# Turning q and k in the second layer by VectorE blocks and a scratch tile in DRAM in place of TensorE

## The chip, the cores and the metric

The kernel runs on one core of a Trainium2 chip. The metric is the device time of one execution in microseconds. Before: 2663.79 us, the median of three runs (2663.64 to 2665.55). Engines are named as in the profile: PE is TensorE's matmul, PEld its weight load, DVE VectorE, ACT ScalarE, POOL GpSimd, SP SyncE, which issues every DMA here.

## The reference, cut to what matters

An encoder trunk of two layers on 256 tokens of width 2048, in float32. In each layer:

```
h = rmsnorm(x) * (1 + sc_a) + sh_a                 # sc_a, sh_a: from c @ ada_w
qa, ka, va, qb, kb, vb, ga, gb = split(h @ w_in)   # qa 8 heads, ka/va 2, qb/kb/vb 8, of 128
qa, ka = rotary(rmsnorm(qa) * qn_a), rotary(rmsnorm(ka) * kn_a)
qb, kb = rmsnorm(qb) * qn_b, rmsnorm(kb) * kn_b
ya = window_attention(qa, ka, va, sink) @ w_proj_a
yb = neighbourhood_attention(qb, kb, vb, bias) @ w_proj_b
x = x + gt_a * ((sigmoid(ga) * ya + sigmoid(gb) * yb) @ w_out)
x = x + gt_m * ffn(x)                              # w_up, conv of width 3, silu gate, w_down
```

Scores are q k^T, so both q and k are wanted with the 128 entries of a head on the partitions and the tokens along the free dimension. The projection leaves them the other way, tokens on the partitions, because the norm of a head and the rotation run along the head's entries. Between the two lies a transposition ("turn") of each 128x128 block: 2 blocks of tokens for each head of q and k. That is what the change touches.

## The kernel before, in words

**Weights.** All weights of a layer stand in DRAM in the order of their use, in units of 16 blocks of 128x128 (1 MB). `unit_steps` (L280) loads a unit (L286) into one of four buffers "raw", and splits it, in two halves of 8 blocks, into a high and a low part: ACT casts (L297), DVE subtracts (L298). The halves are called hl and have four buffers, so two units can lie split ahead. Every product is three matmuls: high by high, high by low, low by high. Loads of ada_w (aw, L225, also 1 MB and also in "raw") stand between those of the units; DVE reduces each against c (L226).

**Order of the work.** `Stream.next_block` (L338) hands out blocks; at the end of each unit `tick` (L331) runs `bg.tick` (L258): first what was deferred at the tick before, then background jobs, each at a rate of steps per tick. The attention of a layer is such a job (L842): one step moves each live head on by one stage and takes in the next head, at 0.4 steps per tick in the second layer (`ATT`, L81). Heads 0 to 7 are those of mixer A, and may start when `ready` (L851) says that the groups they need are turned; the heads of mixer B follow. The program so written is then laid out by a scheduler, engine by engine: each engine has one list that it works off in order, and waits on semaphores for the others. SP's list holds all the DMAs. A DMA holds one of eight semaphores until it has landed.

**The stage of the change.** In the second layer, units 8 to 43 are nine groups of 512 columns of `w_in`, four units each (`Stream.tokens`, L367): group 0 holds k of mixer A (2 heads) and v, 1 and 2 q of mixer A, 3 and 6 k and 5 and 8 q of mixer B with four heads each, 4 and 7 v of mixer B. Units 0 to 7 before and 44 to 51 after them are the gate of mixer A, then comes its projection.

For each group of q or k, `qk_rows` (L539) runs in deferred steps:

- ACT squares each head's rows and sums them (L547), DVE and POOL make the reciprocal roots (L440, L441);
- three ticks later `norm` (L553) scales into the tile qn, 128 tokens x 2 x 4 heads x 128 (L556), and rotates q and k of mixer A (L571 to L573). qn has one buffer;
- one tick later `turn` (L576): for each of two blocks of tokens TensorE transposes each head (L580) into a PSUM tile qtp, and ACT copies that, scaled by the gain, into `dst` (L581), a part of packA or packB. Then `ready` is raised.

**Attention**, `attend` (L602), in stages of one step: q and k are split into high and low (`in_halves`, L588: ACT L389, DVE L390); six matmuls make the scores sc (L607), DVE adds mask or bias and takes the row maxima (L610) and negates them (nm, L615), ACT takes exponentials (L618, with es for the sink, L621), DVE adds and inverts (den L622, ri L624), ACT scales (L626). One step later four transpositions on TensorE (tp, L631), a split of the turned p into pT (L389, L390; one buffer), and one step later six matmuls with v (po, L639) and a split of o (L641, L642). tp, sc, po and qtp share three PSUM buffers "ax". This path of p is as before in both kernels.

Of the kernel before, what the change touches and what calls it, by code (L numbers as in the profile page):

```python
# [15 lines left out]
P = 128  # L16
L = 2
D = 2048
S = 256
# [8 lines left out]
NEG = -1e30  # L28
SCALE = HEAD ** -0.5
GRID_W, NA_KH, NA_KW = 64, 8, 16  # L30


QKV_GROUPS = [1024, 0, 512, 2560, 3584, 1536, 3072, 4096, 2048]
# [48 lines left out]
ATT_B = [0.21, 0.21]  # L82

SCORES_3 = (1,)

ADA_ORDER = [[p * KC + k for k in range(KC) for p in ps] for ps in ((0, 1), (2,), (3, 4), (5,))]
ADA_ORDER = [i for part in ADA_ORDER for i in part]
# [47 lines left out]
def encoder(ctx: ExitStack, tc: tile.TileContext, a: dict, out: bass.AP):  # L135
# [16 lines left out]
    sm = pool("sm", 3)  # L152
    mm = pool("mm", 4, space=bass.MemoryType.PSUM)
    ax = pool("ax", 3, space=bass.MemoryType.PSUM)

    ident = const.tile([P, P], F32, name="ident")
    make_identity(nc, ident[:])
# [228 lines left out]
    def split(dst, src, scale=None):  # L386

        if scale is None:
            nc.scalar.copy(dst[:, 0], src)  # L389
            nc.vector.tensor_tensor(out=dst[:, 1], in0=src, in1=dst[:, 0].bitcast(F32), op=ALU.subtract)  # L390
            return
        nc.scalar.activation(out=dst[:, 0], in_=src, func=AF.Copy, scale=scale)
        nc.vector.scalar_tensor_tensor(
            out=dst[:, 1], in0=src, scalar=scale, in1=dst[:, 0].bitcast(F32), op0=ALU.mult, op1=ALU.subtract
        )
# [140 lines left out]
            nc.vector.tensor_tensor(out=z[:], in0=ps[:, :S], in1=self.rbs[:], op=ALU.mult)  # L536
            return z, sh

    def qk_rows(pss, heads, rot, gain, dst, then):  # L539

        cols = 0
        n = heads * HEAD
        ss = sm.tile([P, 8], F32, name="qss", tag="qss")
        for t, ps in enumerate(pss):
            for i in range(heads):
                sq = at.tile([P, HEAD], F32, name="qsq", tag="qsq", bufs=1)
                nc.scalar.activation(  # L547
                    out=sq[:], in_=ps[:, cols + i * HEAD : cols + (i + 1) * HEAD], func=AF.Square,
                    accum_out=ss[:, t * heads + i : t * heads + i + 1],
                )  # L550
        rs = sm.tile([P, 8], F32, name="qrs", tag="qrs")
        rsqrt(rs[:, : 2 * heads], ss[:, : 2 * heads], HEAD, 2 * heads)
        def norm():  # L553
            qn = at.tile([P, 2, 4, HEAD], F32, name="qn", tag="qn", bufs=1)
            for t, ps in enumerate(pss):
                nc.vector.tensor_tensor(  # L556
                    out=qn[:, t, :heads],
                    in0=ps[:, cols : cols + n].rearrange("p (h d) -> p h d", d=HEAD),
                    in1=rs[:, t * heads : (t + 1) * heads].unsqueeze(2).broadcast_to([P, heads, HEAD]),
                    op=ALU.mult,  # L560
                )
            if rot is not None:
                x1, x2 = qn[:, :, :heads, :HALF], qn[:, :, :heads, HALF:ROT]
                tab = [rot[:, i].unsqueeze(2).broadcast_to([P, 2, heads, HALF]) for i in range(4)]
                tm = []
                for i in range(2):
                    z = ev.tile([P, S], F32, name=f"rt{i}", tag="z")
                    z = z[:].rearrange("p (i t h d) -> p i t h d", i=2, t=2, h=4)
                    tm += [z[:, 0, :, :heads], z[:, 1, :, :heads]]
                for i, src in enumerate((x1, x2, x2, x1)):  # L570
                    nc.vector.tensor_tensor(out=tm[i], in0=src, in1=tab[i], op=ALU.mult)  # L571
                nc.vector.tensor_tensor(out=x1, in0=tm[0], in1=tm[1], op=ALU.subtract)
                nc.vector.tensor_tensor(out=x2, in0=tm[2], in1=tm[3], op=ALU.add)  # L573
            bg.defer(lambda: turn(qn))

        def turn(qn):  # L576
            for t in range(2):
                ps = ax.tile([P, 4, P], F32, name="qtp", tag="ax")
                for h in range(heads):
                    nc.tensor.transpose(ps[:, h], qn[:, t, h], ident[:])  # L580
                nc.scalar.activation(  # L581
                    out=dst[:, :, t * P : (t + 1) * P], in_=ps[:, :heads], func=AF.Identity, scale=gain
                )
            then()

        bg.defer(lambda: bg.defer(lambda: bg.defer(norm)))
# [12 lines left out]

        return ((0, 0), (0, 1), (1, 0))[: 2 * len(x) - 1]  # L600

    def attend(q, k, v, p, mask, scale, sink, o):  # L602

        sc = ax.tile([P, 2, S], F32, name="sc", tag="ax")
        for t in range(2):
            for i, j in by(q):
                nc.tensor.matmul(sc[:, t], q[i][:, t * P : (t + 1) * P], k[j], start=i + j == 0, stop=(i, j) == by(q)[-1])  # L607
        m = sm.tile([P, 2], F32, name="m", tag="m")
        for t in range(2):
            nc.vector.tensor_tensor_reduce(  # L610
                out=p[:, t], in0=sc[:, t], in1=mask[:, t], scale=scale, scalar=-3.0e38 if sink is None else sink,
                op0=ALU.add, op1=ALU.max, accum_out=m[:, t : t + 1],
            )
        nm = sm.tile([P, 2], F32, name="nm", tag="nm")
        nc.vector.tensor_scalar(out=nm[:], in0=m[:], scalar1=-1.0, scalar2=None, op0=ALU.mult)  # L615
        den = sm.tile([P, 2], F32, name="den", tag="den")
        for t in range(2):
            nc.scalar.activation(out=p[:, t], in_=p[:, t], func=AF.Exp, bias=nm[:, t : t + 1], accum_out=den[:, t : t + 1])  # L618
        if sink is not None:
            es = sm.tile([P, 2], F32, name="es", tag="es")  # L620
            nc.scalar.activation(out=es[:], in_=nm[:], func=AF.Exp, bias=sink)  # L621
            nc.vector.tensor_tensor(out=den[:], in0=den[:], in1=es[:], op=ALU.add)  # L622
        ri = sm.tile([P, 2], F32, name="ri", tag="ri")
        nc.vector.reciprocal(out=ri[:], in_=den[:])  # L624
        for t in range(2):
            nc.scalar.activation(out=p[:, t], in_=p[:, t], func=AF.Copy, scale=ri[:, t : t + 1])  # L626
        yield
        tp = ax.tile([P, 2, S], F32, name="tp", tag="ax")
        for k in range(2):
            for t in range(2):  # L630
                nc.tensor.transpose(tp[:, k, t * P : (t + 1) * P], p[:, t, k * P : (k + 1) * P], ident[:])  # L631
        pT = at.tile([P, 2, 2, S], F32R, name="pT", tag="pT", bufs=1)
        split(pT, tp[:])
        v = v()
        yield
        po = ax.tile([P, 512], F32, name="po", tag="ax")
# [121 lines left out]
    for l in range(L):  # L758
# [112 lines left out]
        for pi, (groups, gates) in enumerate(parts):  # L871
            last = pi == len(parts) - 1
            for g, part in enumerate(groups):
                have_h(part)
                pss = st.tokens(h, part)
                if pi == max(0, len(parts) - 2) and g == 0:
                    gains, sink, cw, rots = small(l)
                dst = packs[g // 3][:, 4 * (g % 3) : 4 * (g % 3) + 4]
                rows = dst.rearrange("p (t a) s -> p t (a s)", t=2)
                if not last or pi > 0:  # L880
                    for t, ps in enumerate(pss):
                        if pi == 0:
                            nc.scalar.copy(rows[:, t], ps[:])
                        else:
                            nc.vector.tensor_tensor(out=rows[:, t], in0=ps[:], in1=rows[:, t], op=ALU.add)
                    pss = [rows[:, t] for t in range(2)]
                if not last:
                    continue

                def turned(g=g):  # L890
                    ready[0] = g + 1

                vcol = {0: GA * HEAD, 4: 0, 7: 0}.get(g)
                if vcol is not None and pi == 0:
                    for t in range(2):
                        nc.scalar.copy(rows[:, t, vcol:], pss[t][:, vcol:])
                if g == 0:
                    qk_rows(pss, GA, rots[1], gains[:, 1:2], kTa, turned)
                elif g < 3:
                    qk_rows(pss, 4, rots[0], gains[:, 0:1], dst, turned)  # L900
                elif vcol is None:
                    qk_rows(pss, 4, None, gains[:, 3:4] if g in (3, 6) else gains[:, 2:3], dst, turned)
                else:
                    turned()
                if g == 2:
                    bg.add(job, ATT[l])
# [242 lines left out]
```

## Time and profile before

| | |
|---|---|
| median of 3 runs | 2663.79 us |
| the profiled execution | its page gives a span of 2663.2 us and no time beside it |
| granted TensorE clock | full throughout (9 in all 40 slices) |
| DMA | 700.41 MB in 102,039 packets, mean 263 GB/s |
| packets under 512 B | 12,721 |
| written to DRAM | 2.10 MB, the output |
| chain that ended last | PE 89%, DVE 6%, ACT 1%, DMA 1%, issue 1% |

The profile is of one execution. Times of an instruction are its start from the start of the span and its duration. A busy TensorE is not a TensorE at its peak: matmuls overlap, and the distance from one start to the next tells the rate. "Idle before" in square brackets is time in which that engine had nothing to do, and the arrow names what ended it. The view of the chain of waits follows, from the last instruction back, what each one waited for.

### The profile page before, as it was taken

What the parts mean: (1) busy time and instruction counts of PE and PEld (TensorE: products, weight loads), DVE (VectorE), ACT (ScalarE), POOL (GpSimd) and SP (SyncE); (2) the same over time, 40 slices, a digit from 0 to 9 for tenths busy, and PEclk for the clock granted to TensorE, in tenths of its full rate; (3) what the DMA queues carried; (4) which work ended last, traced back from release to release, by engine and by line L of the source; (5) the groups of instructions that cost most, each with busy time, mean ns of one, the idle gap of its engine ahead of it and who ended that gap; (6) DMA issues with size and microseconds to landing.
All of it is one profiled execution on the core that took longest, in us unless ns stands there. A gap on an engine that the chain in (4) does not pass through costs nothing.

```text
span 2663.2 us, 50845 instructions
## 1 busy us (share of the span) xinstructions
PE 2650.9 (100%) x21256; PEld 2565.7 (96%) x21256; DVE 2102.2 (79%) x2959; ACT 1412.8 (53%) x2284; POOL 36.2 (1%) x25
## 2 busy tenths in 40 slices
PE   9999999999999999999999999999999999999999
PEld 7888899999999999999998889999999999999999
DVE  8898998997987888788976667768888866655664
ACT  5445865456644555355555566554565445544553
POOL 0001100000000000000000000000000000000000
PEclk9999999999999999999999999999999999999999
DMA  9987789885787878788766666666747765555554
GB/s 372 351 327 292 262 300 352 317 320 199 291 294 287 302 288 295 289 294 289 290 217 254 228 229 231 245 252 253 285 173 288 297 256 190 190 194 194 197 191 143
DMA packets 102039, 700.41 MB, mean 263 GB/s; under 512 B 12721, under 2 KB 15025, under 8 KB 17969
## 3 DMA queue, kind: packets, MB, share of 16 engines
q1 hardware_dynamic: 101810, 697.17, 71.4%
q8 instruction: 166, 2.72, 0.4%
q14 instruction: 63, 0.52, 0.1%
HBM read 695.03 MB, written 2.10 MB: 262 GB/s over the span
## 4 chain that ended last, share of the span: by engine, by line
PE 89%; DVE 6%; ACT 1%; issue 1%; DMA 1%; POOL 0%; SPq 0%; DVEq 0%; ACTq 0%
PE ps L314 25%; PE ps L316 25%; PE ps L315 25%; PE ps_t L377 4%; PE ps_t L379 4%; PE ps_t L378 4%; DVE hl L298 2%; DVE aw L226 2%; DMA aw<-in_aw 1%; PE sc L607 1%; PE po L639 1%; ACT hl L297 1%; PE tp L631 1%; POOL qrs L441 0%; PE qtp L580 0%
## 5 line engine op out<-in xcount | busy, mean ns | idle before, releaser
L298 DVE TENSOR_TENSOR hl<-w,hl 128x1024 fp32r<-128x1024 f32 x928 | 1128.3, 1222 | 360.0 <-ACT hl L297 357.6
L297 ACT CAST hl<-w 128x1024 fp32r<-128x1024 f32 x928 | 970.7, 1049 | 748.5 <-PE ps L316 518.1
L314 PE MATMUL ps<-h,hl 128*128 128x256 f32 x3328 | 922.8, 277 | 1.3 <-DVE ya L915 0.6
L315 PE MATMUL ps<-h,hl 128*128 128x256 f32 x3328 | 919.8, 276 | 0.0
L316 PE MATMUL ps<-h,hl 128*128 128x256 f32 x3328 | 919.8, 277 | 0.0
L314 PEld LDWEIGHTS ps<-h,hl 128*128 128x128 f32 x3328 | 624.8, 188 | 2.4 <-DVE ya L915 0.8
L315 PEld LDWEIGHTS ps<-h,hl 128*128 128x128 f32 x3328 | 625.3, 188 | 0.4 <-DVE h L470 0.2
L316 PEld LDWEIGHTS ps<-h,hl 128*128 128x128 f32 x3328 | 624.4, 188 | 0.0
L226 DVE CUSTOM_DVE_ANT_0 aw<-aw,cact,ab 128x2048 f32<-128x2048 f32 x189 | 443.5, 2347 | 48.8 <-DMA aw<-in_aw 47.8
L377 PE MATMUL ps_t<-hl,h 128*128 128x512 f32 x576 | 223.1, 392 | 2.6 <-ACT h L469 2.1
L378 PE MATMUL ps_t<-hl,h 128*128 128x512 f32 x576 | 224.9, 391 | 0.3
L379 PE MATMUL ps_t<-hl,h 128*128 128x512 f32 x576 | 224.3, 390 | 0.0
L994 DVE SCALAR_TENSOR_TENSOR u<-ps,cw,u 128x255 f32<-128x255 f32 x304 | 146.1, 481 | 66.5 <-ACT u L992 62.2
L992 ACT ACTIVATE u<-ps,cw 128x256 f32<-128x256 f32 x152 | 85.9, 565 | 187.9 <-PE ps L316 187.5
L316 PE MATMUL ps<-merged,hl 128*128 128x256 f32 x512 | 141.8, 277 | 0.4 <-DVE hl L298 0.4
L315 PE MATMUL ps<-merged,hl 128*128 128x256 f32 x512 | 141.6, 277 | 0.0
L314 PE MATMUL ps<-merged,hl 128*128 128x256 f32 x512 | 141.6, 277 | 0.0
L315 PE MATMUL ps<-act_o,hl 128*128 128x256 f32 x512 | 141.4, 276 | 0.0
L316 PE MATMUL ps<-act_o,hl 128*128 128x256 f32 x512 | 141.3, 276 | 0.0
L314 PE MATMUL ps<-act_o,hl 128*128 128x256 f32 x512 | 141.2, 276 | 0.0
L377 PEld LDWEIGHTS ps_t<-hl,h 128*128 128x128 f32 x576 | 107.9, 188 | 26.1 <-ACT h L469 3.1
L378 PEld LDWEIGHTS ps_t<-hl,h 128*128 128x128 f32 x576 | 108.1, 188 | 23.7 <-DVE hl L298 1.9
(231 smaller groups left out, 4612.5 us busy)
## 6 DMA issues: line engine op xcount, KB each, us to landing
w<-in_ws SPq DMA_DIRECT2D x463, 1024.0 KB, 4.9
aw<-in_aw SPq DMA_DIRECT2D x189, 1024.0 KB, 6.1
p<-in_bias SPq DMA_DIRECT2D x16, 256.0 KB, 4.2
x<-in_xT SPq DMA_DIRECT2D x4, 512.0 KB, 5.3
aw_o<-in_aw SPq DMA_DIRECT2D x2, 1024.0 KB, 12.3
out<-x SPq DMA_DIRECT2D x16, 128.0 KB, 2.1
w<-in_ws SPq DMA_DIRECT2D x2, 512.0 KB, 11.7
aw_b<-in_aw SPq DMA_DIRECT2D x1, 1024.0 KB, 18.1
```

Of the source, the lines that this page charges most:

```text
L226: nc.vector.tensor_tensor_reduce(out=raw[:], in0=raw[:], in1=cact[:], scale=1.0, scalar=ab[:, i : i + 1], op0=ALU.mult, op1=ALU.add, accum ...
L297: nc.scalar.copy(hl[:, 0], r)
L298: nc.vector.tensor_tensor(out=hl[:, 1], in0=r, in1=hl[:, 0].bitcast(F32), op=ALU.subtract)
L314: nc.tensor.matmul(out, hi, act[0], start=first, stop=False)
L315: nc.tensor.matmul(ps[:, :S], hi, act[1], start=False, stop=False)
L316: nc.tensor.matmul(out, lo, act[0], start=False, stop=last)
L377: nc.tensor.matmul(ps[:], xh, hi, start=kc == kcs[0], stop=False)
L378: nc.tensor.matmul(ps[:], xh, lo, start=False, stop=False)
L379: nc.tensor.matmul(ps[:], xl, hi, start=False, stop=kc == kcs[-1])
L607: nc.tensor.matmul(sc[:, t], q[i][:, t * P : (t + 1) * P], k[j], start=i + j == 0, stop=(i, j) == by(q)[-1])
L992: nc.scalar.activation(out=u, in_=ps, func=AF.Identity, scale=w[:, 1:2], bias=w[:, 3:4])
L994: nc.vector.scalar_tensor_tensor(out=u[:, to], in0=ps[:, of], scalar=w[:, j : j + 1], in1=u[:, to], op0=ALU.mult, op1=ALU.add)
```

## The change

A list `MOVED = (1,)` names the layers of the change, so the first layer stays as it is. In the second layer `turn` no longer uses TensorE and PSUM. For each of the two blocks of tokens VectorE transposes qn in place, which it does in blocks of 32x32, each block for itself. To bring the blocks to their places, eight DMAs per group (two blocks of tokens by four groups of 32 partitions) store qn into a scratch tile qY in DRAM, 128 x heads x 256, in runs of 32 elements (128 B). One tick later one DMA loads qY into `dst`, and one tick after that ACT scales `dst` in place by the gain, and `ready` is raised. The DRAM tile has two buffers. The code for p in `attend` has the same path as an option, which no caller takes. `once` serves that option alone.

```
+BLOCK = 32
+MOVED = (1,)
...
+    dram = pool("dram", 2, space=bass.MemoryType.DRAM)
...
+    def scatter(y, src, t, a):
+
+        rows = y[:].rearrange("(b i) n (t a j) -> t a i n b j", i=BLOCK, t=2, a=P // BLOCK)
+        nc.sync.dma_start(rows[t, a], src[a * BLOCK : (a + 1) * BLOCK])
+
-    def qk_rows(pss, heads, rot, gain, dst, then):
+    def qk_rows(pss, heads, rot, gain, dst, then, moved=False):
...
         def turn(qn):
+            if moved:
+                flat = qn[:, :, :heads].rearrange("p t h d -> p t (h d)")
+                for t in range(2):
+                    nc.vector.transpose(out=flat[:, t], in_=flat[:, t])
+                y = dram.tile([P, heads, S], F32, name="qY", tag="qY")
+                for t in range(2):
+                    for a in range(4):
+                        scatter(y, qn[:, t, :heads].rearrange("p h (b j) -> p h b j", j=BLOCK), t, a)
+
+                def back():
+                    nc.sync.dma_start(dst, y[:])
+
+                    def scaled():
+                        nc.scalar.activation(out=dst, in_=dst, func=AF.Identity, scale=gain)
+                        then()
+
+                    bg.defer(scaled)
+
+                bg.defer(back)
+                return
             for t in range(2):
                 ps = ax.tile([P, 4, P], F32, name="qtp", tag="ax")
...
-                    qk_rows(pss, GA, rots[1], gains[:, 1:2], kTa, turned)
+                    qk_rows(pss, GA, rots[1], gains[:, 1:2], kTa, turned, l in MOVED)
...
-                    qk_rows(pss, 4, rots[0], gains[:, 0:1], dst, turned)
+                    qk_rows(pss, 4, rots[0], gains[:, 0:1], dst, turned, l in MOVED)
```

The two groups of mixer B's q and k are called with `l in MOVED` likewise.

More of the change, by code (lines that the diff above doesn't have):

```diff
@@ L600, in by, with once, run, attend @@
         return ((0, 0), (0, 1), (1, 0))[: 2 * len(x) - 1]
-    def attend(q, k, v, p, mask, scale, sink, o):
+    def once(fn):
+        due = [fn]
+        def run():
+            if due:
+                due.pop()()
+        return run
+    def attend(q, k, v, p, mask, scale, sink, o, moved=False):
         sc = ax.tile([P, 2, S], F32, name="sc", tag="ax")
@@ L627, in attend @@
         yield
-        tp = ax.tile([P, 2, S], F32, name="tp", tag="ax")
-        for k in range(2):
+        if moved:
+            flat = p[:].rearrange("p t k -> p (t k)")
+            nc.vector.transpose(out=flat, in_=flat)
+            y = dram.tile([P, 2, S], F32, name="pY", tag="pY")
             for t in range(2):
-                nc.tensor.transpose(tp[:, k, t * P : (t + 1) * P], p[:, t, k * P : (k + 1) * P], ident[:])
-        pT = at.tile([P, 2, 2, S], F32R, name="pT", tag="pT", bufs=1)
-        split(pT, tp[:])
+                for a in range(4):
+                    scatter(y, p[:, t].rearrange("p (k b j) -> p k b j", k=2, j=BLOCK), t, a)
+            yield
+            pT = at.tile([P, 2, 2, S], F32R, name="pT", tag="pT", bufs=1)
+            whole = pT[:, 1].bitcast(F32)
+            nc.sync.dma_start(whole, y[:])
+            halve = once(lambda: split(pT, whole))
+            bg.defer(halve)
+        else:
+            tp = ax.tile([P, 2, S], F32, name="tp", tag="ax")
+            for k in range(2):
+                for t in range(2):
+                    nc.tensor.transpose(tp[:, k, t * P : (t + 1) * P], p[:, t, k * P : (k + 1) * P], ident[:])
+            pT = at.tile([P, 2, 2, S], F32R, name="pT", tag="pT", bufs=1)
+            split(pT, tp[:])
         v = v()
         yield
+        if moved:
+            halve()
         po = ax.tile([P, 512], F32, name="po", tag="ax")
@@ L897, in encoder @@
                 if g == 0:
-                    qk_rows(pss, GA, rots[1], gains[:, 1:2], kTa, turned)
+                    qk_rows(pss, GA, rots[1], gains[:, 1:2], kTa, turned, l in MOVED)
                 elif g < 3:
-                    qk_rows(pss, 4, rots[0], gains[:, 0:1], dst, turned)
+                    qk_rows(pss, 4, rots[0], gains[:, 0:1], dst, turned, l in MOVED)
                 elif vcol is None:
-                    qk_rows(pss, 4, None, gains[:, 3:4] if g in (3, 6) else gains[:, 2:3], dst, turned)
+                    qk_rows(pss, 4, None, gains[:, 3:4] if g in (3, 6) else gains[:, 2:3], dst, turned, l in MOVED)
                 else:
```

## The prediction

> **What bounds the kernel now.** I read the page first (which engine is full), then the view of busy time by stretches for the second layer's q/k/v stage, then that stage's timeline. In the page's line the columns are busy time, share and instructions; in the stretch view they are the stretch, its length, busy time and count for PE, weight load, DVE, ACT and POOL, granted clock, DMA share and GB/s.
>
> ```profile
> PE 2650.9 (100%) x21256; PEld 2565.7 (96%) x21256; DVE 2102.2 (79%) x2959; ACT 1412.8 (53%) x2284; POOL 36.2 (1%) x25
> 1394.00:1640.00 246.00, 245.94 (x1295) 211.02 (x1294) 165.29 (x251) 144.09 (x308) 10.91 (x7) 1.00 0.65 241
> ```
>
> TensorE is never without work in this stage (245.94 of 246.00 us, clock 1.00), DVE is at 67%, ACT at 59%, the DMA engines at 65%. So whatever leaves TensorE is gained, and whatever makes TensorE wait is lost in full: nothing later has slack to give it back.
>
> ```profile
> 1483.00 0.39 PE L378 MATMUL ps_t<-hl,h 128*128 128x512 f32 x1
> 1483.23 0.39 PE L379 MATMUL ps_t<-hl,h 128*128 128x512 f32 x1
> 1483.46 1.03 PE L580 MATMUL qtp<-ident,qn 128*128 128x128 f32 x8
> 1484.25 0.48 PE L377 MATMUL ps_t<-hl,h 128*128 128x512 f32 x1
> 1484.56 0.39 PE L378 MATMUL ps_t<-hl,h 128*128 128x512 f32 x1
> L580 PE MATMUL qtp<-ident,qn x52: 270/272/273, 1438.5 to 1631.8; 128*128 128x128 f32 x52
> ```
>
> The timeline's first column is the start. Durations overlap; the pitch counts: 0.23 us from one 512-column matmul to the next, so a unit (24 of them in this stage) takes 5.44 us and a group of four units 21.8 us.
>
> **What is removed.** From 1483.46 to 1484.56 there are eight turns and one matmul: 1.10 - 0.23 = 0.87 us for eight, 0.109 each. The last row (instructions of tile qtp in this stage) counts 52. Gain on TensorE: 52 x 0.109 = **5.7 us**, all on the path. [...]
>
> **Durations for what follows**, from the timeline of head 0 of mixer A and its neighbours (start, duration, engine, line):
>
> ```profile
> 1491.86 1.29 DVE L556 TENSOR_TENSOR qn<-ps_t,qrs 128x512 f32<-128x512 f32 x2 [1.81 <-POOL qrs L441]
> 1506.36 0.59 ACT L896 COPY packB<-ps_t 128x512 f32<-128x512 f32 x1
> 1506.95 0.95 PE L607 MATMUL sc<-kA,qA 128*128 128x256 f32 x6
> 1507.94 0.48 DVE L610 CUSTOM_DVE_ANT_0 p<-sc,maskA,sink 128x256 f32<-128x256 f32 x1 [2.00 <-PE sc L607]
> 1508.35 0.48 DVE L610 CUSTOM_DVE_ANT_0 p<-sc,maskA,sink 128x256 f32<-128x256 f32 x1
> 1508.75 2.35 DVE L226 CUSTOM_DVE_ANT_0 aw<-aw,cact,ab 128x2048 f32<-128x2048 f32 x1
> 1511.03 0.17 DVE L615 TENSOR_SCALAR nm<-m 128x2 f32<-128x2 f32 x1
> 1511.10 0.42 DVE L390 TENSOR_TENSOR qA<-packA,qA 128x256 fp32r<-128x256 f32 x1
> 1513.08 0.51 ACT L618 ACTIVATE p<-p,nm 128x256 f32<-128x256 f32 x1
> 1514.08 0.28 ACT L621 ACTIVATE es<-nm,sink 128x2 f32<-128x2 f32 x1
> 1514.39 0.16 DVE L622 TENSOR_TENSOR den<-den,es 128x2 f32<-128x2 f32 x1 [0.60 <-ACT es L621]
> 1514.59 0.17 DVE L624 RECIPROCAL ri<-den 128x2 f32<-128x2 f32 x1
> 1515.21 0.90 ACT L626 ACTIVATE p<-p,ri 128x256 f32<-128x256 f32 x2
> 1516.16 1.05 ACT L297 CAST hl<-w 128x1024 fp32r<-128x1024 f32 x1
> 1517.24 1.23 DVE L298 TENSOR_TENSOR hl<-w,hl 128x1024 fp32r<-128x1024 f32 x1 [0.68 <-ACT hl L297]
> 1518.68 0.60 PE L631 MATMUL tp<-ident,p 128*128 128x128 f32 x4
> 1519.04 0.96 PE L607 MATMUL sc<-kA,qA 128*128 128x256 f32 x6
> 1519.84 0.58 ACT L389 CAST pT<-tp 128x512 fp32r<-128x512 f32 x1
> 1521.11 0.69 DVE L390 TENSOR_TENSOR pT<-tp,pT 128x512 fp32r<-128x512 f32 x1
> ```
>
> The 14 evictions of qtp on ACT go too, and seven scalings in place come (128x1024 each, as the cast at 1516.16: 1.05 us, 7.4 us if nothing covered them). ACT's idle 41% covers them, and I cost them at nothing outside the chains that follow.
>
> **What is added on the queues.** Per group of four heads: two DVE turns of 128x512, which no row shows; below by nothing, above by two of the 2.35 us of a 128x2048 operation, and I take the 128x512 row at 1521.11 (0.69 us), so 1.4 us. Then eight stores of 512 pieces of 128 B, and one load back of 512 rows of 1 KB. In all 6.5 such groups: 26,624 pieces. The nearest row for a store to DRAM is the end of the run, where two stores of 128 rows of 1 KB are alone (the last 8.2 us; 288 packets with their 32 semaphore writes):
>
> ```profile
> q1 hardware_dynamic: 288, 0.26, 9.1%
> out<-x SPq DMA_DIRECT2D x2, 128.0 KB, 1.8
> w<-in_ws SPq DMA_DIRECT2D x463, 1024.0 KB, 4.9
> 1471.37 0.33 SPq L225 DMA_DIRECT2D aw<-in_aw  x1
> 1475.11 5.94 SPq L286 DMA_DIRECT2D w<-in_ws  x3
> ```
>
> So 0.091 x 16 x 8.2 / 288 = 41 ns a packet. A piece of 128 B lies between an eighth of that (5 ns, if bytes count) and 41 ns (if packets count); I take 41, the row of a store. A group's stores are then 4096 x 41 / 16 = 10.5 us of all engines, the load back 1.3 us; over the stage 77 us, against 35% of 246 = 86 us that are free. It fits, closely. SP issues a DMA in 0.33 us, so eight are 2.6 us, beside the transfer.
>
> Where the stores stand on SP matters: in the built program they come before loads that today go ahead of them, and the load back waits until all eight have landed, with the next loads behind it. The loads of units 26 to 28 are issued here from 1475.11 on; in the changed program that of unit 28 stands behind the stores of group 3, whose data exist only after that group's norm (1491.86 above). But unit 28 is due only around 1505 (1484.25 - 0.87 + 21.8), the load lands in 4.9 us, and the joint below makes TensorE later still. Walked through with 10.5 us per group, only unit 23 comes late by itself. Its load stands behind group 1's stores:
>
> ```profile
> 1446.37 1.29 DVE L556 TENSOR_TENSOR qn<-ps_t,qrs 128x512 f32<-128x512 f32 x2 [1.53 <-POOL qrs L441]
> 1448.70 0.89 DVE L571 TENSOR_TENSOR rt<-qn,rot 128x128 f32<-128x128 f32 x4
> ```
>
> In the new DVE list, from 1446.37 on: norm 1.3, rotation 1.4, one reduction of aw 2.35, four subtractions 4.9 and two turns 1.4, together 11.3: the second turn ends at 1457.7. Stores begin after the first turn, near 1456, and have landed near 1468.5 (10.5 and 1.8). The load back and unit 23's load leave then and land near 1475; cast and subtraction (1.05 + 1.23) make 1477.3, and the unit is due at 1476.7 (1483.46 - 5.44 - 1.3 for the turns gone): late by about **1 us**. The other loads are late by less than the waits that come next, and hide behind them.
>
> **What is moved: the attention steps.** This is the large term. The engines run their lists in order, and the lists of the changed kernel are another mix. TensorE's, with the number of matmuls:
>
> ```
> before: units 24-27, turns x8, sc0 x6, 28, 29, tp0 x4, sc1 x6, 30, 31, 32,
>         po0 x6, tp1 x4, sc2 x6, 33, 34, po1, tp2, sc3, 35 ...
> after:  unit 23 with sc0 x5 inside, 24, sc0 x1, tp0 x1, sc1 x3, 25 (sc1 x1 inside), tp0 x3, sc1 x2,
>         26 (po0 x2 inside), 27, po0 x4, tp1 x4, sc2 x6, po1 x6, tp2 x1, sc3 x3, tp2 x3, sc3 x3, 28, po2, 29-37,
>         tp3, sc4, po3, 38, 39, tp4, sc5, po4, tp5, sc6, po5 x2, 40 (po5 x4 inside), tp6, sc7,
>         41 (po6 x2 inside) ...
> ```
>
> Before, two or three units (11 to 16 us) lie between the scores of a head (sc), its turn (tp) and its product (po). After, whole heads stand back to back at the joints 24/25, 27/28, 37/38 and 39/40, and the DVE and ACT lists hold the split of the next unit's weights (hl) *behind* the softmax of the last head. What one head takes is in the rows of head 0 above. On TensorE tp takes 0.36 us (1518.68 to 1519.04), and sc and po, six matmuls each, about 0.8. Each joint's wait is the chain to the next unit's first hl, less TensorE's own work in it:
>
> - 24/25. Unit 24's end frees sc0's last matmul; then second reduction 0.48, qA and nm 0.5, group 3's norm 1.29 and its two DVE turns 1.4 (they stand ahead in DVE's list; ACT's exponentials run beside them), den and ri 0.37, scaling 0.45, cast 1.05, subtraction 1.23: 6.8, less 0.6 of tp and sc: **6.2 us**.
> - 25/26. A reduction 0.48 and the subtraction 1.23 behind it: 1.7; inside unit 26 po0 waits for pT behind a second subtraction, 1.23 + 0.69 - 0.45: 1.5. **3.2 us**.
> - 27/28. Two evictions 1.2 (L896), one o copy 0.4 (as qA's), pT 0.58 + 0.69, two reductions 0.9, qA and nm 0.5, exponentials with es 1.28 (1513.08 to 1514.36), den and ri 0.37, scaling 0.90, cast 1.05, subtraction 1.23: 9.1 plus about 0.5 for the hand-overs, less 3.6 of TensorE's work: **6.0 us**.
> - 28/29. pT, aw's 2.35, three small ones and the split in DVE's list against 5.44 + 0.8 of TensorE: **1.6 us**.
> - 37/38. pT 1.3, two reductions 0.9, subtraction 1.23, behind tp: 4.0 less 1.7: **2.3 us**.
> - 39/40. As 27/28, with a second pT (0.69) ahead of the split: 10.4 less 3.4: **7.0 us**.
> - 40/41. aw's reduction stands ahead of den: scaling, split and po6's pT come **3.3 us** late.
>
> Sum 29.6, with unit 23's 1 us 30.6, less 5.7 gained: **+24.9 us** on the profiled execution's span of 2663.2 us, so 2688.1. The median of the runs shown, 2663.79, is 0.6 above that span; added, **2689 us**. These are chains put together from one execution; each may be off by a third, and the loads could arrive during the joints later than walked.
>
> **The rivals.**
>
> *Pieces dearer than any row* (the queue becomes the bound). At 82 ns, twice the dearer end, the stores and loads back are 136 + 9 = 145 us beside 160 us (0.65 x 246) of the present traffic: the stage would need 305 us, 59 more, and the joints' waits disappear in that: 2663.8 + 59, some 2723 us. For it: SP sends one queue in order, and 128 B is far below every load's row. Against: nothing in the trace shows a small store costing more than a large one. [...]
>
> *The turns leave and nothing waits* (the other side). The place is TensorE's list, the price -5.7 us: 2658.1. It decides once the joints' waits stay below 0.4 us in all, which needs softmax, turn and product of a head to follow within the 3.6 us of matmuls at 27/28. Head 0's rows speak against it: from 1513.08 to 1516.11 alone are exponentials and scaling.
>
> *Half the joints.* If the waits of the two joints without a full softmax (25/26, 37/38) and half of the others don't appear, 12 us stay: 2663.8 + 12 + 1 - 5.7 = 2671.
>
> **How the numbers follow.** Forecast (2689, with its waits uncertain by a third: 2679 to 2699) 0.60; dearer pieces 0.17; half the joints 0.15; nothing waits 0.03; in between, waits and gain about equal, 0.05. A measurement of this kernel can tell about 0.2%, 5.3 us, from no change. The range goes from 2671 (the half case in) to 2724 (the dear case in). Faster 0.03, same 0.05, slower 0.92.
>
> **What would show it.** Right: in the profile after, TensorE falls below 100% in the stage only at the joints named, with idle time ended by DVE's hl and ACT's pT; no qtp row; the stage's DMA share near 0.9. The pieces' price shows in the queue's packets and its share. Wrong: idle TensorE ended by loads (w) spread over the stage means the dearer pieces; a TensorE without gaps means that the joints' chains run beside more than I saw. A stretch longer outside 1394 to 1700 would be a cause that I missed altogether.

## The result, and the profile after

The changed kernel takes 2687.07 us (median of 4, 2685.47 to 2688.46), the kernel before, beside it on the same chip, 2663.93 us: 23.1 us more, ratio 1.0084 (95% interval 1.007 to 1.0097). The forecast was 2689. It hits the time and the places. Two of its large terms are wrong, though, and that they cancel is luck; the section after the experiments takes them one by one.

The page of the changed kernel (span 2686.4 us of an execution of 2688.46), and the view by stretches for the stage of the change, with the columns of before:

```profile
PE 2660.2 (99%) x21204; PEld 2568.8 (96%) x21204; DVE 2108.7 (78%) x2973; ACT 1411.1 (53%) x2277; POOL 37.6 (1%) x25
```

```profile
1394.00:1640.00 246.00, 231.15 (x1052) 190.53 (x1051) 155.77 (x239) 132.02 (x279) 12.08 (x7) 0.95 0.69 238
w<-in_ws SPq DMA_DIRECT2D x40, 1024.0 KB, 6.4
```

The last line is from the view of the DMAs from 1394 to 1663: loads, KB each, median from issue to landing. The 52 turns are gone (21256 to 21204 matmuls). In the stage TensorE stands idle for 14.85 us of 246, where it had 0.06. The DMA share rose from 0.65 to 0.69 only. A load of weights lands somewhat later than before, 6.4 us after its issue against 5.3 in the same window. One number was not there before at all: the granted clock is 0.95, not 1.00.

What ended TensorE's idle time from 1394 to 1700 (us in all, times, longest), and its gaps of 0.8 us and more in the timeline:

```profile
PE tp L683 <- ACT p L664: 10.3, 3, 4.8
PE ps_t L382 <- DVE hl L302: 3.6, 4, 1.2
PE po L693 <- DVE pT L394: 0.7, 3, 0.2
```

```profile
1493.93 0.47 PE L683 MATMUL tp<-ident,p 128*128 128x128 f32 x1 [4.77 <-ACT p L664]
...
1505.18 0.50 PE L382 MATMUL ps_t<-hl,h 128*128 128x512 f32 x1 [1.19 <-DVE hl L302]
...
1521.74 0.33 PE L683 MATMUL tp<-ident,p 128*128 128x128 f32 x1 [2.79 <-ACT p L664]
...
1525.41 0.79 PE L382 MATMUL ps_t<-hl,h 128*128 128x512 f32 x1 [0.87 <-DVE hl L302]
...
1526.00 0.63 PE L383 MATMUL ps_t<-hl,h 128*128 128x512 f32 x1
...
1528.98 0.47 PE L382 MATMUL ps_t<-hl,h 128*128 128x512 f32 x1
```

```profile
1602.27 0.47 PE L683 MATMUL tp<-ident,p 128*128 128x128 f32 x1 [2.79 <-ACT p L664]
...
1617.25 0.50 PE L382 MATMUL ps_t<-hl,h 128*128 128x512 f32 x1 [1.02 <-DVE hl L302]
```

These are the joints that the prediction named: 24/25 at 1493.93, 25/26 at 1505.18, 27/28 at 1521.74 and 1525.41, 39/40 at 1602.27, inside unit 41 at 1617.25. No gap is ended by a load. What a reader should not overlook are the rows *without* brackets. From 1526.00 to 1528.98 are seven steps from one matmul to the next: a pitch of 0.426 us, where 0.227 is usual. TensorE counts as busy there, at half its pace. The stretches say the same in their granted clock. Three are slow; around the wait of 1.2 us at 1505.18 the clock stays at 1.00:

```profile
1491.60:1498.43 6.83, 4.50 (x13) 3.48 (x14) 5.23 (x8) 5.65 (x10) 0.00 (x0) 0.50 0.77 201
1500.00:1520.00 20.00, 17.55 (x86) 14.04 (x85) 9.53 (x22) 8.37 (x20) 0.00 (x0) 1.00 0.61 229
1522.32:1529.15 6.83, 5.96 (x18) 4.47 (x17) 5.42 (x8) 3.78 (x6) 0.00 (x0) 0.50 0.22 65
1600.82:1611.06 10.24, 8.61 (x27) 7.06 (x28) 6.68 (x13) 6.68 (x16) 0.00 (x0) 0.50 0.13 38
```

The account of the 23.1 us: -5.7 for the turns, +14.9 idle, so +13.9 in time in which TensorE counts as busy. In the slow stretches it was busy for 4.50 + 5.96 + 8.61 = 19.1 us at half its clock, and half of that, 9.5 us, is lost. The other 4.4 us are not split further; waits short enough to vanish under the modelled ends of matmuls are my guess for them, which no run shows. The pitch, 0.426 us against 0.227, fits the granted 0.50; waits of 2.8 us, to 1521.74 and to 1602.27, were enough here.

### The profile page after: what moved, and what is told of

Its sections match the earlier page's. It is cut to its first block, busy times and chain, and to the rows that moved or that the text cites. A ratio compares the mean times of both kernels' runs of the same rounds, so it can differ in the third digit from the quotient of the medians.

```text
span 2686.4 us, 50829 instructions
## 1 busy us (share of the span) xinstructions
PE 2660.2 (99%) x21204; PEld 2568.8 (96%) x21204; DVE 2108.7 (78%) x2973; ACT 1411.1 (53%) x2277; POOL 37.6 (1%) x25
## 4 chain that ended last, share of the span: by engine, by line
PE 92%; DVE 4%; ACT 2%; DMA 1%; issue 1%; POOL 0%; SPq 0%; DVEq 0%; ACTq 0%
PE ps L318 26%; PE ps L320 26%; PE ps L319 26%; PE ps_t L382 4%; PE ps_t L383 4%; PE ps_t L381 4%; DVE hl L302 1%; DVE aw L230 1%; ACT hl L301 1%; PE sc L645 1%; DMA w<-in_ws 1%; PE po L693 1%; PE tp L683 1%; ACT qsq L556 0%; ACT p L656 0%
## 5 line engine op out<-in xcount | busy, mean ns | idle before, releaser
L382 PE MATMUL ps_t<-hl,h 128*128 128x512 f32 x576 | 228.0, 396 | 4.0 <-DVE hl L302 3.6
L381 PE MATMUL ps_t<-hl,h 128*128 128x512 f32 x576 | 224.8, 397 | 2.6 <-ACT h L473 1.6
L383 PE MATMUL ps_t<-hl,h 128*128 128x512 f32 x576 | 226.6, 394 | 0.0
```

The lines of the kernel that those rows point to most:

```text
L381: nc.tensor.matmul(ps[:], xh, hi, start=kc == kcs[0], stop=False)
L382: nc.tensor.matmul(ps[:], xh, lo, start=False, stop=False)
L383: nc.tensor.matmul(ps[:], xl, hi, start=False, stop=kc == kcs[-1])
```

## The experiments

All times are set against the kernel before on the same chip and beside it, by ratio with its 95% interval; the difference in us is that of the medians. The theory was **order**: the attention steps stand back to back in TensorE's list. The rival was **transfers**: the 128-B stores, or their place in SyncE's queue, make the weights late.

| kernel | ratio | us more than before |
|---|---|---|
| changed kernel | 1.0084 (1.007 to 1.0097) | 23.1 |
| a_pin: its TensorE list in the written order | 1.0034 (1.0022 to 1.0047) | 8.8 |
| e2: before, with dead stores | 1.0057 (1.0043 to 1.007) | 15.0 |
| e4: before, with bunched steps | 1.0081 (1.0065 to 1.0096) | 21.5 |
| e5: e4 with a filler of 9 us | 1.009 (1.0076 to 1.0104) | 24.0 |
| e6: e4 with a filler as long as the wait | 1.0062 (1.0045 to 1.0078) | 17.2 |
| e7: e4 and e2 together | 1.0079 (1.0063 to 1.0095) | 20.6 |
| f_after_pool: stores on GpSimd's queue | 1.0337 (1.0322 to 1.0353) | 90.9 |
| f_act: a_pin, stores on ScalarE's queue | 1.0126 (1.0111 to 1.0141) | 33.0 |
| g_defer2: a_pin, stores two units later | 1.0016 (1.0002 to 1.0029) | 4.5 |
| e8: e2 with 2-KB pieces | 1.0005 (0.9993 to 1.0017) | 1.5 |
| h_loads: a_pin, loads first on SyncE | 0.9991 (0.9982 to 0.9999) | -2.5 |
| h_loads_casts: h_loads, splits first too | 1.001 (1.0001 to 1.0019) | 2.8 |

g_defer2, f_act and e8 ran on a chip on which the kernel before took 2682.05 us; only their ratios compare with the others.

**Order put right: a_pin.** Every matmul of the second layer's units, and of sc, tp and po, is held in the written order; so there is one attention step per two or three units.

```
+    def pe(l, ins):
+        return tc.keep_in_program_order(ins) if l else ins
...
-        nc.tensor.matmul(out, hi, act[0], start=first, stop=False)
+        pe(l, nc.tensor.matmul(out, hi, act[0], start=first, stop=False))
```

> The changed kernel with everything it does (DVE turns, 128-B stores, load back), but TensorE's list in the second layer's q/k/v stage is held in the order in which the program was written: one attention step every two or three units, as in the kernel before, not several back to back. Theory (order): the waits at the joints and the slow clock after them go, the 5.7 us of turns stay gained: about 2658 us, 5 to 6 below the kernel before, no TensorE gap over 1 us and clock 1.00 in all stretches from 1394 to 1700. Rival (the stores and their place in SP's queue delay the weights): the stores are the same, so it stays near the changed kernel, 2680 to 2687 us, and the idle time is ended by loads or by hl.

2673.43 us: 8.8 more than before, so 14.3 less than the changed kernel, each against its own neighbour. Neither theory is right alone. Its waits in the same stretch:

```profile
PE ps_t L386 <- DVE hl L306: 4.4, 3, 2.5
PE ps_t L385 <- ACT hl L305: 3.1, 2, 1.6
PE tp L687 <- ACT p L668: 0.9, 1, 0.9
```

The turn of p hardly waits any more; now the splits of the weights are late, 7.5 us in five gaps. ACT's timeline shows both forms of it:

```profile
1493.99 2.00 ACT L305 CAST hl<-w 128x1024 fp32r<-128x1024 f32 x2 [4.92 <-DMA w<-in_ws]
...
1507.59 1.27 ACT L954 COPY packB<-ps_t 128x512 f32<-128x512 f32 x2 [9.00 <-PE ps_t L387]
1508.75 1.99 ACT L305 CAST hl<-w 128x1024 fp32r<-128x1024 f32 x2
```

At 1493.99 a cast waits for its load, with TensorE not yet waiting for the cast. At 1508.75 one stands in ACT's list behind an eviction that waits for TensorE, and TensorE, at 1509.85, for the cast. I take it that the lists are built to the late loads; h_loads below bears on that.

**Order alone: e4.** The kernel before, without any new transfer, its TensorE list held in the written order as in a_pin; two whole steps stand back to back before units 28 and 40, one or none before the others.

```
+STEPS = {24: 1, 25: 1, 26: 1, 28: 2, 31: 1, 37: 1, 40: 2, 42: 1, 45: 1, 48: 1, 50: 1}
...
             bg.tick()
+            if self.l:
+                for _ in range(STEPS.get(self.u, 0)):
+                    next(now[1])
```

> The kernel before without any new transfer and with its turns on TensorE; only the attention steps are issued elsewhere: two whole steps back to back before unit 28 and two before unit 40, the other units one or none. Theory (order): each pair makes TensorE wait some 3 to 5 us for one softmax and the next split, and the clock row shows less than 1.00 for the next 8 us, some 3 us more each: 10 to 15 us in all, 2674 to 2679 us. Rival (the transfers): no transfer is added, so no change, 2662 to 2666 us.

2686.06 us, more than expected: not only the two pairs, also a single step ahead of them, at 1499.41, makes TensorE wait. The order alone, with the turns where they were, costs as much as the whole change.

```profile
1499.41 1.15 PE L643 MATMUL tp<-ident,p 128*128 128x128 f32 x4 [2.51 <-ACT p L638]
...
1518.10 1.25 PE L651 MATMUL po<-pT,vA 128*128 128x256 f32 x6 [1.75 <-DVE oA L654]
...
1522.27 1.30 PE L643 MATMUL tp<-ident,p 128*128 128x128 f32 x4 [2.92 <-ACT p L638]
1523.22 1.63 PE L619 MATMUL sc<-kA,qA 128*128 128x256 f32 x6
1524.65 0.63 PE L389 MATMUL ps_t<-hl,h 128*128 128x512 f32 x1
1525.08 0.63 PE L390 MATMUL ps_t<-hl,h 128*128 128x512 f32 x1
```

**The clock's share: e5 and e6.** Matmuls on the identity, whose results are not used, keep TensorE busy while a pair waits.

```
+        if fill[i]:
+            wt = ax.tile([P, 512], F32, name="warm", tag="ss", bufs=1)
+            for _ in range(fill[i]):
+                tc.keep_in_program_order(nc.tensor.matmul(wt[:, :P], ident[:], ident[:], start=True, stop=True))
```

> As the kernel with the two bunched pairs, plus 40 matmuls of 128x128 on the identity at the place where each pair waits (their results are not used), so that TensorE is busy during the wait: 40 x 0.06 to 0.11 = 2.4 to 4.4 us of filler per pair. If the clock drops because TensorE stands idle and this costs time of its own, the clock stays at 1.00 and the time is 4 to 8 us below the bunched kernel, 2668 to 2672 us. If only the wait costs time, it is equal to the bunched kernel or up to 2 us above it.

2688.58 us: a miss. An f32 product of 128x128 shows as two instructions here, 0.111 us from start to start, so the 40 were 80 and took 9.1 us, about twice the wait. The clock did stay up (1.00 from 1514 to 1534, where e4 has 0.83), and with 8.8 us of filler beyond the waits of the two pairs the kernel takes only 2.5 us more than e4, on the same chip. To show it more plainly, the filler was cut to the wait:

> As the kernel with the two bunched pairs (2686.1 us), with a filler cut to the length of the two waits: 8 f32 matmuls of 128x128 after the scores of the first step of a pair and 13 ahead of the turn of the second, by the 0.111 us of each of their two passes 1.8 and 2.9 us against waits of 1.75 and 2.92 us (their results are not used). If the slow clock costs time of its own, some 2.8 us a pair come back: 2679 to 2682 us, with pitch 0.23 us right behind each pair. If it costs nothing beside the wait, 2685 to 2688 us.

2682.11 us, some 4 us less than e4, though TensorE does useless work in the same time; the samples don't overlap (2681.19 to 2682.81 against 2685.71 to 2686.72). They come from two chips, on which the kernel before differs by 0.3 us, and the intervals of the two ratios overlap; the traces say how the 4 us come about. The same place in e6:

```profile
1515.20 1.95 PE L624 MATMUL warm<-ident 128*128 128x128 f32 x16
...
1518.31 3.07 PE L624 MATMUL warm<-ident 128*128 128x128 f32 x26
...
1522.10 0.94 PE L632 MATMUL sc<-kA,qA 128*128 128x256 f32 x6
1522.88 0.39 PE L394 MATMUL ps_t<-hl,h 128*128 128x512 f32 x1
1523.10 0.40 PE L395 MATMUL ps_t<-hl,h 128*128 128x512 f32 x1
```

The scores behind the wait take 0.94 us and not 1.63, the pitch of the unit behind them is 0.23 and not 0.43. In e4 the granted clock is 0.83 from 1514 to 1534 and from 1594 to 1614, which at half speed is 6.8 us in each. The pitch is back at 0.23 us behind 1527.21 and 1609.00, so the slow time begins within the waits that end at 1522.27 and 1604.91, and by this estimate TensorE is busy for some 5.0 and 4.3 us of it. In e6 the clock is 1.00 in both stretches. Half of the busy time is 4.7 us, about what e6 gives back. So the slow clock costs time of its own: some 2 us for each pair, on top of 4.7 us of idleness.

**Transfers alone: e2, e7 and e8.** e2 is the kernel before, in its own order, with the eight stores of each group and a load back into qn, for which nothing waits; the turns read qn first.

```
+            if now[0]:
+                y = dram.tile([P, heads, S], F32, name="qY", tag="qY")
+                for t in range(2):
+                    for a in range(4):
+                        scatter(y, qn[:, t, :heads].rearrange("p h (b j) -> p h b j", j=BLOCK), t, a)
+                flat = qn[:].rearrange("p t h d -> p (t h d)")[:, : heads * S]
+                bg.defer(lambda: nc.sync.dma_start(flat, y[:].rearrange("p h s -> p (h s)")))
```

> The kernel before, with its turns on TensorE and its own TensorE order, plus the same number of 128-B stores (eight per group, of data that nothing reads afterwards) and a load back per group into a tile that nothing reads: transfers that are added for their cost alone. Theory (order): about the time before, 2662 to 2667 us. Rival (the transfers): the 20 us and more of the changed kernel appear here too, about 2680 to 2690.

2679.62 us: 15.0 more. But the experiment has a flaw, which SyncE's timeline shows: the load back overwrites qn, so it waits for TensorE's turns, which the changed kernel's does not, and the weights behind it wait too.

```profile
1502.02 0.55 SPq L293 DMA_DIRECT2D w<-in_ws  x1
1513.05 0.33 SPq L603 DMA_DIRECT2D qn<-qY  x1
```

From 1502.6 to 1513.05 SyncE stands at the load back. The longest gap is none the less a joint, this time in ACT's list: unit 28's cast stands behind head 0's exponentials, though its load left at 1502.02.

```profile
1516.54 0.28 ACT L640 ACTIVATE es<-nm,sink 128x2 f32<-128x2 f32 x1
1516.72 1.03 ACT L304 CAST hl<-w 128x1024 fp32r<-128x1024 f32 x1
```

```profile
1517.80 0.79 PE L384 MATMUL ps_t<-hl,h 128*128 128x512 f32 x1 [4.08 <-ACT hl L304]
```

So e2 shows what a blocked SyncE queue costs, with the lists that are built to it, not what the stores cost by themselves. In e7, e4's bunched steps and e2's transfers are put together:

> The bunched pairs (alone 21.5 us more than before) and the dead stores with the dead load back on SyncE's queue (alone 15.0 us more), turns still on TensorE: both costs of the changed kernel without its gain. If the two add up, 2664.6 + 36.5 = 2701 us. If late weights hide behind the joints' waits, as the prediction had it, between 2686 and 2692 us; the changed kernel itself, with the 5.7 us gain taken off it, stands at 2693.

2685.48 us, which is e4's time: what costs 15 us alone costs nothing beside the bunched order. Late loads hide behind the joints. In e8 the stores have the same bytes in pieces of 2 KB:

```
-                        scatter(y, qn[:, t, :heads].rearrange("p h (b j) -> p h b j", j=BLOCK), t, a)
+                        whole(y, qn[:, t, :heads], t, a)
...
+        rows = y[:].rearrange("p n s -> p (n s)").rearrange("p (t h d) -> p t h d", t=2, d=P)
+        at_ = slice(a * BLOCK, (a + 1) * BLOCK)
+        nc.sync.dma_start(rows[at_, t], src[at_])
```

> The kernel before with dead stores as in the run with 128-B pieces (2679.6 us), with the same bytes and number of stores but 32 pieces of 2 KB in each instead of 512 of 128 B (32 and up to 2 KB for the first group); in SyncE's list some loads change place with stores by one. If the small pieces are the cost (their issue, 0.6 us each, and their time on the DMA engines), it vanishes: 2664 to 2668 us. If the cost is that SyncE waits at the stores for their data, it stays: 2674 to 2682 us.

1.0005: the cost is gone. I can't call that the piece size alone, since in SyncE's list some loads now stand ahead of the load back that blocked e2. It stays inconclusive; the pieces' price comes from the trace instead, below. The run shows one thing more: e2, e4 and e8 all hold TensorE's order, and here the hold costs nothing.

**The place in SyncE's list: g_defer2, h_loads, h_loads_casts.** In g_defer2 the stores of a_pin are written two units later.

```
+                def out():
                     y = dram.tile([P, heads, S], F32, name="qY", tag="qY")
...
-                bg.defer(back)
+                    bg.defer(back)
+
+                bg.defer(lambda: bg.defer(out))
```

> The kernel with the pinned order (2673.4 us), with the eight stores of a group written two units later in the program, so that in SyncE's list one to three of the weights' loads that stood behind them come ahead and the stored data are ready when SyncE reaches them. Theory (place in SyncE's list: loads wait behind stores whose data come late): most of the 8.4 us of TensorE's waits go, 2660 to 2667 us. Rival (the transfers themselves, 3.4 us of all engines and 5.3 us of issuing per group, push the loads back wherever they stand): 2671 to 2676 us.

1.0016, about half of a_pin's excess, though the intervals overlap. One event is left, and it is such a joint in ACT's list: the cast of unit 30 stands behind a softmax.

```profile
1539.91 0.91 ACT L671 ACTIVATE p<-p,ri 128x256 f32<-128x256 f32 x2 [0.49 <-DVE ri L669]
1540.73 1.97 ACT L305 CAST hl<-w 128x1024 fp32r<-128x1024 f32 x2
```

```profile
1541.81 0.79 PE L385 MATMUL ps_t<-hl,h 128*128 128x512 f32 x1 [5.41 <-ACT hl L305]
```

In h_loads the stores stay where a_pin has them, and the weights' loads go first:

```
-            nc.sync.dma_start(raw[:], a["ws"][l, u])
+            with urgent(l and 18 <= u <= 72):
+                nc.sync.dma_start(raw[:], a["ws"][l, u])
```

> The kernel with the pinned order (1.0034 of the kernel before), with the weights' loads of units 18 to 72 put first wherever SyncE's list can choose: three loads then stand ahead of a group's load back and the next group's stores, where one or two stood behind them. Nothing else is edited; the stores are the same 26,624 pieces. Theory (place in SyncE's list): TensorE's waits for hl go for the most part and the turns' gain shows, ratio 0.998 to 1.000. Rival (the transfers and their issuing, wherever they stand): 1.002 to 1.005 as before.

2662.26 us, 2.5 less than before and 11.3 less than a_pin, by this edit alone, each against its own neighbour. SyncE from 1475 on in a_pin, and from 1460 on in h_loads:

```profile
1475.16 5.28 SPq L550 DMA_DIRECT2D qY<-qn  x8
1480.54 0.56 SPq L294 DMA_DIRECT2D w<-in_ws  x1
...
1483.05 0.97 SPq L294 DMA_DIRECT2D w<-in_ws  x2
...
1498.65 0.55 SPq L294 DMA_DIRECT2D w<-in_ws  x1
```

```profile
1460.49 8.97 SPq L295 DMA_DIRECT2D w<-in_ws  x3
...
1474.69 5.28 SPq L551 DMA_DIRECT2D qY<-qn  x8
...
1480.73 5.99 SPq L295 DMA_DIRECT2D w<-in_ws  x3
```

```profile
1394.00:1640.00 246.00, 244.77 (x1284) 210.04 (x1284) 172.81 (x256) 141.28 (x295) 10.86 (x7) 1.00 0.76 262
```

The stores start at about the same time, when their data are there. In a_pin the loads of units 25 to 27 stand behind them, and that of unit 28, at 1498.65, behind the next group's stores too. In h_loads unit 25's has left before them, as the third of the first line, and unit 28's, the third of the last line, leaves before the next group's stores, which start at 1491.49: each 11 to 12 us earlier. The stage has one gap of 1.23 us, clock 1.00, and carries the same pieces at a DMA share of 0.76. So the transfers themselves cost little: -5.7 for the turns and 1.2 of idleness would make -4.5, and -2.5 was measured (interval -4.8 to -0.3). The loads' place in the queue was the larger cost, with what ACT's and DVE's lists make of it, which came out otherwise in h_loads too and which no run separates. This kernel beats both: 0.9991 (0.9982 to 0.9999), a gain at the edge of what can be measured. No run puts the loads first in the kernel before, so how much of that gain belongs to the change is not shown. With the splits put first as well:

> As the kernel with the loads first, and the casts and subtractions of the same weights put first in ACT's and DVE's lists too, so that a unit's split no longer stands behind a head's softmax there. If what is left of the waits is such joints in the lists of ACT and DVE: ratio 0.997 to 0.999, no TensorE gap over 0.5 us, clock 1.00 throughout the stage. If it is late data: the same as the kernel with the loads first, or worse where a cast that has to wait for its load stands ahead of a softmax.

1.001, worse by the case named there: ahead of one head's scaling (L670) stand casts, and one wait appears, of 3.29 us at 1664.66 for that scaling, behind which the clock falls to 0.91 from 1654 to 1674.

**Another queue: f_after_pool and f_act.** In f_after_pool the changed kernel's stores and load back are issued by GpSimd (`nc.gpsimd.dma_start` in `scatter` and `back`), with no order held; TensorE's list comes out with one step per two or three units by itself.

> The changed kernel with one edit: the stores to the scratch tile and the load back of q and k go to GpSimd's queue, not SyncE's. Theory (place): the cost lies in SyncE's list, where the weights' loads stand behind stores whose data come late, and in the order that the lists take on because of it; in the built program TensorE's list has one attention step every two or three units again. Then the 5.7 us of turns show: about 2658 to 2661 us, clock 1.00 and no TensorE gap over 1 us. Rival (the transfers themselves): the same 26,624 pieces still pass through the same DMA engines, so the weights stay late as with the pinned order, about 2670 to 2676 us. Third possibility: GpSimd issues such stores slowly or the next norm's rqs on GpSimd waits behind them, and then TensorE waits for hl or for q and k, over 2680 us.

2755.83 us, the third possibility. GpSimd's timeline for the second group, and two waits from 1394 to 1760 (us in all, times, longest):

```profile
1479.91 0.74 POOL L546 DMA_DIRECT2D qY<-qn  x1 [1.89 <-issue]
1482.55 0.74 POOL L546 DMA_DIRECT2D qY<-qn  x1 [1.91 <-issue]
```

```profile
ACT packB L599 <- DMA packB<-qY: 76.9, 4, 22.6
PE ps_t L381 <- ACT hl L301: 38.7, 4, 15.4
```

A store every 2.6 us or more, where SyncE has one every 0.66. The load back is late, ACT stands at the scaling that needs it, with casts of weights behind, and TensorE waits mostly for split weights, not for q and k. In f_act they go to ScalarE's queue:

> The kernel with the pinned order, with the stores and the load back on ScalarE's queue, not SyncE's. Theory (place): SyncE's list is free of them, as with GpSimd's queue, and ScalarE issues them as fast as SyncE does, 0.6 us each: 5 us of a group's 21.8 us, which ScalarE's idle 41% covers if its casts are not late behind the wait for the second DVE turn: 2660 to 2668 us. Rival: ScalarE's list stands at the stores until the turns are done and the casts behind them are late, as the weights' loads were on SyncE: 2672 us and more, with TensorE waiting for hl that ACT casts late without a load ending ACT's idle time.

1.0126, the rival. ScalarE issues as fast as SyncE (0.65 us at the median, SyncE 0.63 in a_pin), but its squares and casts stand behind the wait for the store's data:

```profile
1475.96 8.49 ACTq L550 DMA_DIRECT2D qY<-qn  x8
1484.57 0.28 ACT L560 ACTIVATE qsq<-ps_t 128x128 f32<-128x128 f32 x1 [14.38 <-DMA qY<-qn]
```

## Why the prediction was right, and where its steps were wrong

- **Bound.** Right: TensorE is full in the stage, and every stop is paid in full.
- **Turns, -5.7 us.** Not measured alone. h_loads fits it: 2.5 us gained with 1.2 us of idleness left. So does a_pin against e2, 6.2 us apart, though e2's flaw lies in that. As the kernel before was not run with its loads first, neither isolates the term.
- **DVE turns.** Right: 0.69 each was taken, the row has 1.29 for two.

```profile
1491.74 1.29 DVE L589 STREAM_TRANSPOSE qn<-qn 128x512 f32<-128x512 f32 x2
```

- **Pieces at 41 ns.** Wrong by three. From 1643.9 to 1649.2 of the changed kernel almost nothing but stores is under way (packets, MB, share):

```profile
q1 hardware_dynamic: 3173, 0.40, 50.3%
```

  0.503 x 16 x 5.3 / 3173 = 13.4 ns a piece, 3.4 us of all engines for a group and not 10.5. So the DMA share did not come near 0.9. The row taken as nearest gave the price of a packet of 1 KB, and 41 ns for that is 5 ns for each 128 B: the piece lies between the two bounds, nearer to the one by bytes. (The load back is 128 packets of 4 KB, not 512 of 1 KB; its bytes are the same.) The rival of dearer pieces falls with this. A piece does cost more than its share of a large load: by the queue's row of before from 1394 to 1663 (63.67 MB at 64.3% of 16 engines in 269 us) 128 B take 5.6 ns there.
- **SyncE's issue at 0.33 us.** Wrong by two: the store of 512 pieces has 0.57 to 0.63.

```profile
L546 SPq DMA_DIRECT2D qY<-qn x56: 569/627/1394, 1425.2 to 1648.6; - x56
```

  Eight take 5.3 us and more, longer than the engines need. Issuing, not the engines, sets the pace of the stores.
- **Unit 23 late by 1 us.** Not seen; no gap lies near 1476.
- **Other loads hide behind the joints.** Right: e7 equals e4. But it hid a second cost: without the joints, the loads' place in the queue is worth 11.3 us (a_pin to h_loads). The rival "nothing waits" had the joints as its only condition, and a_pin comes near it (0.9 us at tp for the changed kernel's 10.3) and is still 8.8 us slower than the kernel before. Its time comes about only once the loads go first, and then not in full.
- **The joints, +29.6 us.** The mechanism and the places are right: a_pin, which undoes the order alone, gives back 14.3 us, and e4, which does it alone, costs 21.5. The size is wrong: 14.9 us of idleness, half. At 24/25, 4.8 us came for 6.2, at 25/26 1.2 for 3.2, at 27/28 3.9 for 6.0 (with 0.2 at po), at 37/38 0.8 for 2.3, at 39/40 3.0 for 7.0 (with 0.2 at po), inside unit 41 1.0 for 3.3, at 28/29 none for 1.6. The chains added durations one behind the other, which in part ran side by side, and most waits ended earlier, at the softmax's scaling (10.3 us, tp), not at the split behind it.
- **The clock.** Missed altogether: no term for the slower TensorE behind a wait. It is 9.5 of the 13.9 us beyond the idle time; e6 shows the effect by itself.

So the forecast's sum came out by luck, through two errors of about the same size: some 16 us too much idleness (30.6 against 14.9), and 14 us of lost pace left out, 9.5 of them the slow clock. Idle time was what the rival "half the joints" said, and its 2671 was wrong because it had no lost pace either. What share of the changed kernel's 23.1 us belongs to the order and what to SyncE's queue can't be split for good, since each hides the other (e4 21.5, e7 20.6); in the order in which they were undone, it is 14.3 for TensorE's order and 11.3 for the loads' place, and -2.5 stays.

## What to carry to other kernels

Before costing a transfer, look at what stands *behind* it in its queue: here stores of 13.4 ns a piece cost 11 us because loads stood behind them, and letting the loads go first returned it. Price a stop of a full TensorE with the pace afterwards: where waits of 3 to 5 us took the clock down, they cost 2 to 4 us more, and the busy column won't show it, but the pitch and the granted clock do. And when two delays end in the same wait, undo both before calling either harmless.

## What the runs showed of the hardware

- In the changed kernel a wait of 1.2 us left the clock at 1.00; waits of 2.8 us (each with one of 0.2 us close ahead) and 4.8 us dropped it to 0.50, and the slow pitch lasted 4.5 to 8.7 us from the wait's end (to 1498.42 and to 1610.97).
- The length of a wait alone does not decide: one of 2.5 us left the clock at 1.00 in a_pin (to 1491.82; 1.00 from 1474 to 1494, pitch 0.23 us behind it) and dropped it in e4 (to 1499.41; 0.91 from 1494 to 1514, pitch 0.43 us). In the changed kernel the slow stretches last 6.83, 6.83 and 10.24 us, and TensorE stood idle for 2.4, 2.8 and 1.6 us in the 3.4 us ahead of each. What else decides, no run here shows.
- SyncE took 0.33 us in the median to issue a load of 1 MB (before), 0.42 for a store of 32 pieces of 2 KB (e8), and 0.57 to 0.63 for one of 512 pieces of 128 B (the changed kernel).
- GpSimd's queue took 2.6 us and more for each store of 512 pieces (f_after_pool), at least four times SyncE's 0.66. Eight of these stores, 3.4 us of all engines in the changed kernel by the estimate above, took longer than that to issue: 5.3 us on SyncE, 24 on GpSimd for the group above (1459.33 to 1483.29).
- A matmul of two f32 tiles of 128x128 shows as two instructions, 0.111 us from start to start (160 rows for the 80 of e5); the f32 turn of the same size is one (52 rows for 52 in before).
